# The end of a linear recurrence: a third panel over the finished channels, weights split into freed rooms, and the first evictions of the next stage

## The chip, the core and the metric

The kernel runs on one core of a Trainium2 chip. The metric is the device time of one execution in microseconds (us). A core has a matrix engine (TensorE, PE in the profile; PEld are its weight loads), a vector engine (VectorE, DVE), an activation engine (ScalarE, ACT), a general engine (GpSimd, POOL) and an engine that here only issues DMAs (SyncE, SP). They run side by side and wait for each other by semaphores; each takes its own instructions in order.

## What is computed

One layer of a streaming encoder, for a prompt of 1024 rows and a sample of 64 rows, which the kernel handles together as T = 1088 columns of transposed activations. Cut to what matters here:

```
z = rms_norm(x) @ w_in                      # xa, ga, q, k, v, gb, fl, ma, mb
ua = causal_conv(xa)                        # branch A, 1024 channels
r, i = sigmoid(blockdiag(ua) ...)
a = exp(-8 * r * softplus(-a_param))
h[t] = a[t] * h[t-1] + sqrt(1 - a[t]**2) * (i * ua)[t]     # the recurrence
ya = h * silu(ga)
yb = attention(q, k, v, forget) * silu(gb)  # branch B
u  = [ya @ w_branch[0], yb @ w_branch[1]]
mix = (sigmoid(ma) * u[0] + sigmoid(mb) * u[1]) @ w_o      # then norms, residual, a second small mix
```

All products are made in three passes of matmuls: each float32 operand is split into a high half (rounded on ACT) and a low half (the rest), and hi*hi, lo*hi and hi*lo are added up in one accumulator. So a weight panel is used only after a split: one ACT instruction writes wh, one DVE instruction writes wl.

## The kernel before

Channels of branch A are handled in eight tiles of 128 (k = 0 to 7, KT = 8). Weights come in panels of 128 output channels over eight tiles of input channels; over the 1088 columns a panel is three chunks of 364, 364 and 360 columns (CH), so 3 x 8 x 3 = 72 matmuls, and a chunk is 24. Each chunk has one accumulator; from the recurrence on there are eight of them, one PSUM bank each, taken in turn (`mm`, tag "acc").

`panel()` (L292) hands out the next panel in a fixed list: it asks for weights to be loaded when there is room (`look_ahead`, L257), splits them (`split_next`, L279), and also splits the panel after that, ahead of time. Raw weights lie in `w_raw`: two panels of branch A or B come as a pair in one load of four DMAs on SP, and the next pair is asked for only when both panels of the last are split. Split panels lie in wh and wl of `wpool`, two rooms each, so a new split waits for the matmuls of the panel two before it.

Recurrence (L1549 to L1642): for each k, a projection panel x (input), a panel g (SiLU gate), two small block matrices (`gate`, six accumulators gacc), then on ACT exponentials, tanh and a square root (`decay`, `root`), on DVE products and a scan (`state_in`, `scan`), the product with the gate (`output`), and the split of the result into ya[k] (`split_y`: yah on ACT, yal on DVE). The order on ACT and DVE is that of the code here (`manual_schedule`); PE's order is that of the code throughout. On POOL and SP, and on ACT and DVE behind L1642, a scheduler orders by its own estimate.

At the recurrence's end (k = 6 and 7) the code goes: the gate matmuls of 6, g6, the last merge-gate panel f (L1612, `fill`, evicted by `spill`: ACT copies to `st`, then stores to d_mb), the gate matmuls of 7 between f's first and second chunk, then g7 (L1620 and L1632). Behind it stand two panels of branch A's output projection that are held open (`Held`, L1532): a0 is taken at L1626 and a1 at L1644, each with three accumulators; they run over channels 0 to 4, then over channel 5, 6 and 7 as these get done. Channels 5, 6 and 7 (below y5, y6, y7) are split into rooms of tiles that the recurrence has finished with.

Then stage A (L1677): for of = 0 to 7, panel a_of over all channels, evicted by `evac_a`: DVE multiplies by the merge gate sigmoid(ma), which `gate_in` loads and passes through ACT one panel ahead, and SP stores to d_mix. `branch_b(of)` beside it makes one tile of branch B's y: two loads on SP (yb_in and gb_in, 544 KB each), a sigmoid on ACT, a product on POOL, one on DVE, then a split on ACT and DVE. Then stage B takes panels b0 to b7 over those.

The pools p3 (recurrence) and xpool are closed at L1649, and p4 and ybpool (stage A) take their memory: a tile there waits for the last use of what it lies over.

Of the kernel before, what the change touches and what calls it, by code (L numbers as in the profile page):

```python
# [7 lines left out]
F32 = mybir.dt.float32  # L8
F32R = mybir.dt.float32r
# [56 lines left out]
def hybrid_step(tc, a, o):  # L66
# [137 lines left out]
    def chunk(steps):  # L204
        for _ in range(KT):
            next(steps)
# [69 lines left out]
            for tag, raw in zip(tags, raws_):  # L276
                ahead.append([tag if isinstance(tag, tuple) else ("r", tag), raw, None, False, len(tags)])

    def split_next(eng):  # L279
        if ahead and ahead[0][2] is None:  # L280
            raw = ahead[0][1]
            wh = wpool.tile([P, KT, P], F32R, name="wh")
            wl = wpool.tile([P, KT, P], F32R, name="wl")
            copy_act(wh[:, :, :], raw)
            if ahead[0][0][0] in "xgf":
                copy_act(wl[:, :, :], f(wh[:, :, :]), -1.0)
                pool.dma_start(wl[:, :, :], raw, accum_op=ALU.add)
            else:
                sub(eng, wl[:, :, :], raw, f(wh[:, :, :]))
            ahead[0][2:4] = (wh, wl), True  # L290

    def panel(eng=None):  # L292

        look_ahead()
        if not ahead:
            return None
        split_next(eng or dve)
        tag, _, w, *_ = ahead.popleft()
        look_ahead()
        split_next(eng or dve)  # L300
        look_ahead()
        return tag, w

    def spill(dst, t0, n, z, s=None):
        s = s or wpool.tile([P, GC], F32, name="st")
        copy_act(s[:, :n], z)
        act.dma_start(dst[:, t0:t0 + n], s[:, :n])
# [1224 lines left out]
    class Held:  # L1532


        def __init__(self, want, xs):
            got, self.w = panel()
            assert got == want
            self.xs = xs
            self.accs = [mm.tile([P, 512], F32, name="held", tag="acc") for _ in CH]

        def part(self, ks, evac=None):
            for c, (t0, n) in enumerate(CH):
                for k in ks:
                    three(self.accs[c][:, :n], self.w[0][:, k, :], self.w[1][:, k, :],
                          self.xs[k][0][:, t0:t0 + n], self.xs[k][1][:, t0:t0 + n], k == 0, k == KT - 1)
                if evac:
                    evac(c, t0, n, self.accs[c][:, :n])
# [64 lines left out]
    tag, w = panel()  # L1612
    assert tag == ("f", KT - 1)
    fill = panel_steps(mm, *w, xs, lambda c, t0, n, z: spill(d_mb[KT - 1], t0, n, z))
    early_gate(k - 1)
    output(k - 1)
    chunk(fill)
    gate(k + 1)
    run(fill)
    ga = own_gate(k + 1)  # L1620
# [2 lines left out]
    decay(k + 1)  # L1623
    decay_a(k + 1)
    mix_u(k + 1)
    first = [Held(("a", 0), ya)]  # L1626
    root(k)
    root(k + 1)
    set_sigmoid()
    state(k)  # L1630
    output(k)
    run(ga)  # L1632
    state_in(k + 1)
    ya.append((shared('u', F32R, 'yah5'), shared('r', F32R, 'yal5')))
    split_y(5)
# [5 lines left out]
    split_y(7)  # L1641
    seq.__exit__(None, None, None)  # L1642
    first[0].part(range(5))
    first.append(Held(("a", 1), ya))  # L1644
    first[1].part(range(5))
    for i in (5, 6):
        for h in first:
            h.part([i])
    p3.close()  # L1649
    xpool.close()  # L1650

# [16 lines left out]
        sub(dve, l[:, :], t[:, :], f(h[:, :]))  # L1668

    def gate_in(pl, src):  # L1670
        g = pl.tile([P, T], F32, name="gate", tag="gate", bufs=2)
        sp.dma_start(g[:, :], src)
        act.activation(out=g[:, :], in_=g[:, :], func=AF.Sigmoid)
        return g

    g_next = gate_in(p4, d_ma[0])
    for of in range(KT):  # L1677
        g = g_next
        if of + 1 < KT:
            g_next = gate_in(p4, d_ma[of + 1])  # L1680

        def evac_a(c, t0, n, z):
            s = wpool.tile([P, GC], F32, name="st")
            dve.tensor_tensor(out=s[:, :n], in0=z, in1=g[:, t0:t0 + n], op=ALU.mult)
            sp.dma_start(d_mix[of][:, t0:t0 + n], s[:, :n])

        if of < 2:
            first[of].part([KT - 1], evac_a)
        else:
            tag, w = panel()  # L1690
            assert tag == ("a", of)
            run(panel_steps(mm, *w, ya, evac_a))
        branch_b(of)
        if of == 2:
            ft_p = mm.tile([P, 512], F32, name="ft_p", tag="acc")
            pe.transpose(ft_p[:64, :P], fin.rearrange("p s k -> p (s k)"), ident[:, :])
# [509 lines left out]
```

## Time and profile before

| | us |
|---|---|
| median of 3 runs (lowest, highest) | 1464.6 (1464.26, 1467.74) |
| the profiled execution | 1467.15 |
| its span | 1465.4 |
| mean granted TensorE clock over the span | 0.994 |

The profile is of one execution, so its times are compared with its own 1467.15 us. A row of a group of instructions gives the line in the code, the engine, the operation, written tile <- read tiles with shapes, the count, busy time and the mean of one; a row of the timeline begins with start and duration in us, and brackets at its end give how long the engine idled before it and what it waited for. Matmuls are pipelined: in an undisturbed stretch one of 364 columns is shown with 0.33 us and the next one starts 0.17 us later. The recurrence's end and the start of stage A lie between about 1010 and 1100 us of the span.

### The profile page before, as it was taken

The page shows a single profiled execution, that of the slowest core. Times are in us where ns is not written, and L with a number is a line of the kernel's source. Part 1 is how long each engine was busy: PE and PEld are TensorE (multiplying, and loading weights), DVE is VectorE, ACT ScalarE, POOL GpSimd, SP SyncE. Part 2 cuts the span into 40 slices and gives each one's busy share as a digit, 9 for nine tenths or more (in the row PEclk, how much of TensorE's full clock was granted, in tenths as well). Part 3 has the DMA queues.
Part 4 walks back from the last instruction along what each step waited for, and adds up shares of the span by engine and source line. Part 5 has one row for each costly group of instructions (what it writes and reads, how often), then busy time and mean ns, then how long its engine had stood idle before and what let it go on. Part 6 is the DMA issues. An engine that isn't in the chain of part 4 may idle for free.

```text
span 1465.4 us, 25652 instructions
## 1 busy us (share of the span) xinstructions
PE 1436.0 (98%) x9653; PEld 1394.7 (95%) x9653; DVE 893.7 (61%) x1631; ACT 717.1 (49%) x1353; POOL 299.1 (20%) x385
## 2 busy tenths in 40 slices
PE   8999999999999999999999999999999999999997
PEld 8999999999999999999899989999999999879997
DVE  5464866564325666666466555898755574778534
ACT  4423444442215566666456556777444232554633
POOL 0013324323123332333233210221023000000001
PEclk9999999999999999999999999999999999999999
DMA  8457456754276565646545344454278774224111
GB/s 285 143 119 109 130 163 189 181 178 127 78 210 157 120 148 139 141 112 139 118 129 128 61 108 70 86 101 84 99 235 273 257 218 152 100 86 171 43 43 44
DMA packets 149304, 200.64 MB, mean 137 GB/s; under 512 B 24212, under 2 KB 115836, under 8 KB 148156
## 3 DMA queue, kind: packets, MB, share of 16 engines
q1 hardware_dynamic: 129772, 167.06, 44.2%
q10 hardware_dynamic: 17680, 25.64, 5.1%
q0 software_dynamic: 1728, 6.29, 2.3%
q8 instruction: 76, 1.25, 0.4%
q14 instruction: 48, 0.39, 0.1%
HBM read 131.04 MB, written 65.80 MB: 134 GB/s over the span
## 4 chain that ended last, share of the span: by engine, by line
PE 84%; DVE 7%; ACT 4%; DMA 3%; issue 2%; SPq 0%; POOL 0%; ACTq 0%; DVEq 0%; POOLq 0%
PE quad L805 17%; PE acc L170 12%; PE acc L172 12%; PE acc L171 12%; PE q L1853 5%; PE tp L1147 4%; PE pv L1175 2%; PE s L1125 2%; PE s L1126 2%; PE pv L1177 2%; PE vacc L170 1%; PE vacc L171 1%; PE vacc L172 1%; PE vacc L471 1%; PE q L1978 1%
## 5 line engine op out<-in xcount | busy, mean ns | idle before, releaser
L170 PE MATMUL acc<-xh,wh 128*128 128x364 f32 (+1 forms) x768 | 253.2, 330 | 1.3 <-ACT st L82 1.2
L171 PE MATMUL acc<-xl,wh 128*128 128x364 f32 (+1 forms) x768 | 252.0, 328 | 0.0
L172 PE MATMUL acc<-xh,wl 128*128 128x364 f32 (+1 forms) x768 | 251.8, 328 | 0.0
L170 PEld LDWEIGHTS acc<-xh,wh 128*128 128x128 f32 x768 | 144.9, 189 | 2.6 <-ACT st L82 1.9
L171 PEld LDWEIGHTS acc<-xl,wh 128*128 128x128 f32 x768 | 144.7, 188 | 0.5
L172 PEld LDWEIGHTS acc<-xh,wl 128*128 128x128 f32 x768 | 144.5, 188 | 0.0
L1105 DVE CUSTOM_DVE_ANT_0 s<-s,mask 128x1024 f32<-128x1024 f32 (+7 forms) x128 | 95.5, 767 | 26.8 <-PE s L1126 26.7
L85 DVE TENSOR_TENSOR wl<-w_raw,wh 128x1024 fp32r<-128x1024 f32 (+1 forms) x54 | 62.6, 1160 | 67.3 <-ACT wh L82 66.3
L1110 POOL TENSOR_SCALAR pb<-pb,sm 128x896 f32<-128x896 f32 (+1 forms) x64 | 61.8, 966 | 196.2 <-DVE sm L1109 178.2
L82 ACT ACTIVATE wh<-w_raw 128x1024 fp32r<-128x1024 f32 (+1 forms) x66 | 64.3, 976 | 65.6 <-PE quad L805 27.3
L85 DVE TENSOR_TENSOR tl<-tp,th 128x512 fp32r<-128x512 f32 x96 | 65.7, 688 | 35.6 <-ACT th L82 35.6
L805 PE MATMUL quad<-xh,wh 128*128 128x272 f32 x384 | 80.7, 291 | 0.0
L805 PE MATMUL quad<-xl,wh 128*128 128x272 f32 x384 | 79.5, 288 | 0.0
L805 PE MATMUL quad<-xh,wl 128*128 128x272 f32 x384 | 79.4, 288 | 0.0
L82 ACT ACTIVATE th<-tp 128x512 fp32r<-128x512 f32 x96 | 56.9, 596 | 40.6 <-PE tp L1147 33.4
L1107 ACT ACTIVATE pb<-s,nm 128x896 f32<-128x896 f32 (+1 forms) x64 | 61.1, 954 | 30.0 <-DVE nm L1105 27.7
L1125 PE MATMUL s<-k,q 128*128 128x256 f32 (+1 forms) x192 | 67.1, 353 | 0.2 <-ACT pb L1107 0.2
L1147 PE MATMUL tp<-ident,pb 128*128 128x128 f32 x416 | 63.9, 274 | 1.2 <-DVE diag0l L85 0.7
L1126 PE MATMUL s<-k,q 68*128 68x256 f32 (+1 forms) x192 | 65.0, 350 | 0.0
L171 PE MATMUL acc<-ybl,wh 128*128 128x364 f32 (+1 forms) x192 | 62.9, 328 | 0.0
L172 PE MATMUL acc<-ybh,wl 128*128 128x364 f32 (+1 forms) x192 | 62.8, 327 | 0.0
L170 PE MATMUL acc<-ybh,wh 128*128 128x364 f32 (+1 forms) x192 | 62.7, 326 | 0.0
(705 smaller groups left out, 4151.8 us busy)
## 6 DMA issues: line engine op xcount, KB each, us to landing
w_raw<-in_w_in SPq DMA_DIRECT2D x56, 256.0 KB
q<-d_q SPq DMA_DIRECT2D x48, 256.0 KB
k<-d_k SPq DMA_DIRECT2D x48, 256.0 KB
w_raw<-in_w_in SPq DMA_DIRECT2D x64, 128.0 KB
w_raw<-in_w_branch SPq DMA_DIRECT2D x32, 256.0 KB
wl<-w_raw POOLq DMA_DIRECT2D x12, 512.0 KB, 4.6
wraw<-in_w_in SPq DMA_DIRECT2D x20, 256.0 KB
d_k<-oh ACTq DMA_DIRECT2D x16, 272.0 KB
```

The source lines that it names most:

```text
L82: return act.activation(out=out, in_=in_, func=AF.Copy, scale=scale)
L85: return eng.tensor_tensor(out=out, in0=in0, in1=in1, op=ALU.subtract)
L170: pe.matmul(out, ah, bh, start=start, stop=False)
L171: pe.matmul(out, ah, bl, start=False, stop=False)
L172: pe.matmul(out, al, bh, start=False, stop=stop)
L805: pe.matmul(acc[:, c, :CW], l[:, k, :], r[:, k, c * CW:(c + 1) * CW], start=(first and k == 0 and p == 0), stop=(k == 3 and p == 2), skip_ ...
L1105: at = book("D", now[0] + HOP_PE, per(D_MAX, n), lambda: dve.tensor_tensor_reduce(out=s[:, :n], in0=s[:, :n], in1=m, scale=-1.0, scalar=-N ...
L1110: return free, book("G", at, per(G_NORM, n), lambda: pool.tensor_scalar(out=pr[:, :n], in0=pr[:, :n], scalar1=sm, scalar2=1.0, op0=ALU.mul ...
L1125: pe.matmul(s[:, c0:c0 + w], t["q1"][:, q0:q0 + P], t["k1"][:, c0:c0 + w], start=True, stop=False)
L1126: pe.matmul(s[:, c0:c0 + w], t["q2"][:HD + 4, q0:q0 + P], t["k2"][:HD + 4, c0:c0 + w], start=False, stop=True)
L1147: pe.transpose(tp[:, o0 + i * P:o0 + (i + 1) * P], pr[par][:, kb * P:(kb + 1) * P], ident[:, :])
L1853: pe.matmul(acc, l[:, k, :], r[:, k, :], start=(first and k == 0 and i == 0), stop=(k == 3 and i == 2), skip_group_check=not first)
```

## The change

It has five parts.

1. f's first chunk (`chunk(fill)`) is written ahead of `early_gate` and `output` of channel 5, so that its eviction stands ahead of theirs on ACT and DVE.
2. `panel` may be given rooms for the panel that it splits ahead, and told not to split ahead. With a0, a1 is now split into the rooms uh and ul of p3 (inputs of the gate matmuls), no longer into wpool.
3. a1 and a2 are both taken inside the written order, behind g7 and ahead of `state_in(7)`; so a2 is split there too. a2 is held as well, with two accumulators, and its first two chunks run over channels 0 to 4, then 5, 6 and 7 with a0 and a1. `Held` takes an accumulator only when a chunk begins; a2's third chunk runs whole in stage A.
4. In stage A's first step, a3 is split and the pair a4 and a5 is asked for behind a0's last matmuls.
5. Evictions of stage A go to st_a of p4 with four rooms (before: st of wpool with two), and merge gates are loaded two panels ahead with three rooms (before: one ahead with two).

```diff
-    def split_next(eng):
+    def split_next(eng, rooms=None):
...
-            wh = wpool.tile([P, KT, P], F32R, name="wh")
-            wl = wpool.tile([P, KT, P], F32R, name="wl")
+            wh, wl = rooms or (wpool.tile([P, KT, P], F32R, name=n) for n in ("wh", "wl"))
...
-    def panel(eng=None):
+    def panel(eng=None, rooms=None, split=True):
...
-        split_next(eng or dve)
+        if split:
+            split_next(eng or dve, rooms)
...
-            self.accs = [mm.tile([P, 512], F32, name="held", tag="acc") for _ in CH]
-
-        def part(self, ks, evac=None):
-            for c, (t0, n) in enumerate(CH):
+            self.accs = {}
+
+        def part(self, ks, evac=None, cs=range(len(CH))):
+            for c in cs:
+                t0, n = CH[c]
+                if c not in self.accs:
+                    self.accs[c] = mm.tile([P, 512], F32, name="held", tag="acc")
...
+    chunk(fill)
     early_gate(k - 1)
     output(k - 1)
-    chunk(fill)
...
-    first = [Held(("a", 0), ya)]
+    rooms = [p3.tile([P, W_SC], F32R, name=n, tag=n)[:, :D].rearrange("p (k n) -> p k n", k=KT) for n in ("uh", "ul")]
+    first = [Held(("a", 0), ya, rooms=rooms)]
...
     run(ga)
+    first.append(Held(("a", 1), ya))
+    first.append(Held(("a", 2), ya, split=False))
     state_in(k + 1)
...
     first[0].part(range(5))
-    first.append(Held(("a", 1), ya))
     first[1].part(range(5))
+    first[2].part(range(5), cs=(0, 1))
     for i in (5, 6):
-        for h in first:
+        for h in first[:2]:
             h.part([i])
+        first[2].part([i], cs=(0, 1))
...
-        g = pl.tile([P, T], F32, name="gate", tag="gate", bufs=2)
+        g = pl.tile([P, T], F32, name="gate", tag="gate", bufs=3 if pl is p4 else 2)
...
-    g_next = gate_in(p4, d_ma[0])
+    g_ahead = deque(gate_in(p4, d_ma[i]) for i in range(2))
...
-            s = wpool.tile([P, GC], F32, name="st")
+            s = p4.tile([P, GC], F32, name="st_a", bufs=4)
...
         if of < 2:
             first[of].part([KT - 1], evac_a)
+            if of == 0:
+                split_next(dve)
+                look_ahead()
+        elif of == 2:
+            first[2].part([KT - 1], evac_a, (0, 1))
+            first[2].part(range(KT), evac_a, (2,))
```

How this moves instructions is seen in the built programs. First ACT, around the gate matmuls of channel 7; wh and wl are g7's weights, st is f's first chunk on its way out, q the sigmoid for channel 5's gate:

```order
 L82 ACTIVATE wh<-w_raw 128x1024
 L82 ACTIVATE wl<-wh 128x1024
+L82 ACTIVATE st<-acc 128x364
+L307 DMA d_mb<-st 128x364
 L1529 ACTIVATE q<-sg_e 128x1088
-L82 ACTIVATE st<-acc 128x364
-L307 DMA d_mb<-st 128x364
 L1444 ACTIVATE x_e<-gacc,vt 128x364 x3
```

The eviction and its store have moved ahead of the sigmoid. Next DVE, from channel 7's input product (x_e) to the last low half of y (the third yal is y7's). Before, where the first wl is a1's and the last a2's:

```order
L1450 TENSOR_TENSOR x_e<-x_e,u_e 128x1092
L85 TENSOR_TENSOR wl<-w_raw,wh 128x1024
L1478 SCALAR_TENSOR_TENSOR r<-e,r 128x1092
L1479 TENSOR_TENSOR x<-x,r 128x1092
L1480 COPY x<-vt 128x1
L1485 SCALAR_TENSOR_TENSOR e<-q,x 128x1092
L1503 TENSOR_TENSOR sg<-e,sg 128x1024
L1504 TENSOR_TENSOR sg<-e,sg 128x64
L1517 TENSOR_TENSOR sg_e<-acc,sg_e 128x364 x2
L1517 TENSOR_TENSOR sg_e<-acc,sg_e 128x360
L1478 SCALAR_TENSOR_TENSOR r_e<-e_e,r_e 128x1092
L1479 TENSOR_TENSOR x_e<-x_e,r_e 128x1092
```

And now, from the product with g7 on, where the first wl is a2's and the second a3's:

```order
L1517 TENSOR_TENSOR sg_e<-acc,sg_e 128x360
L85 TENSOR_TENSOR wl<-w_raw,wh 128x1024
L1478 SCALAR_TENSOR_TENSOR r_e<-e_e,r_e 128x1092
L1479 TENSOR_TENSOR x_e<-x_e,r_e 128x1092
L1480 COPY x_e<-vt 128x1
L85 TENSOR_TENSOR yal_12386<-xp,yah_12385 128x1088
L1485 SCALAR_TENSOR_TENSOR e_e<-q_e,x_e 128x1092
L1503 TENSOR_TENSOR r<-e_e,sg_e 128x1024
L1504 TENSOR_TENSOR r<-e_e,sg_e 128x64
L85 TENSOR_TENSOR yal_12396<-sg,yah_12395 128x1088
L85 TENSOR_TENSOR yal_12400<-r,yah_12399 128x1088
L85 TENSOR_TENSOR wl<-w_raw,wh 128x1024
```

a2's low half has come in ahead of channel 7's state; in a1's place, behind the first x_e, stands the same instruction with ul and uh for wl and wh. On ACT the high halves stand likewise: uh directly behind the tanh of channel 7, a2's wh ahead of y5's high half, and a3's behind y7's. Behind a3's low half DVE goes on with the first evictions into st_a. Third, SP at the start of stage A, with the semaphores that each request waits for. Before:

```order
L1672 DMA gate<-d_ma 128x1088 [waits DVE_49,PE_49,Pool_49]
L1672 DMA gate<-d_ma 128x1088
L1661 DMA yb_in<-d_y 128x1088 [waits DMAHW3_49]
L1662 DMA gb_in<-d_gb 128x1088 [waits DMAHW4_49,DVE_49]
L1685 DMA d_mix<-st 128x364 [waits DMAHW5_49,DVE_49]
```

And now:

```order
L1679 DMA gate<-d_ma 128x1088 [waits DVE_49,PE_49,Pool_49]
L1679 DMA gate<-d_ma 128x1088 [waits PE_49]
L1679 DMA gate<-d_ma 128x1088 [waits DMAHW3_49]
L1668 DMA yb_in<-d_y 128x1088 [waits DMAHW4_49,DVE_49,PE_49]
L1692 DMA d_mix<-st_a 128x364 [waits DMAHW5_49,DVE_49]
L1692 DMA d_mix<-st_a 128x364 [waits DMAHW6_49,DVE_49]
L1692 DMA d_mix<-st_a 128x360 [waits DMAHW7_49,DVE_49]
L254 DMA w_raw<-in_w_branch 128x2x256 [waits DMAHW0_49,Activation_49]
L254 DMA w_raw<-in_w_branch 128x2x256 [waits DMAHW1_49]
L254 DMA w_raw<-in_w_branch 128x2x256 [waits DMAHW2_49]
L254 DMA w_raw<-in_w_branch 128x2x256 [waits DMAHW3_49]
L1669 DMA gb_in<-d_gb 128x1088 [waits DMAHW4_49]
```

The second gate has gained a wait for PE: its room lies over uh, which a1's matmuls read to their end. Three gates now stand ahead of yb_in, and the first gb_in has moved behind a0's stores and the weights of a4 and a5. The DMAHW names stand for eight lanes that SP's requests take in turn; a request waits for the one eight before it. PE's order has the 30 matmuls of a2's first two chunks over channels 0 to 4 behind a1's, and 6 each for channels 5, 6 and 7; the rest of a2 follows behind a1's last matmuls.

More of the change, by code (lines that the diff above doesn't have):

```diff
@@ L1532, in hybrid_step, with __init__ @@
     class Held:
-        def __init__(self, want, xs):
-            got, self.w = panel()
+        def __init__(self, want, xs, **kw):
+            got, self.w = panel(**kw)
             assert got == want
             self.xs = xs
-            self.accs = [mm.tile([P, 512], F32, name="held", tag="acc") for _ in CH]
-        def part(self, ks, evac=None):
-            for c, (t0, n) in enumerate(CH):
+            self.accs = {}
[4 more added lines that the diff above has]
+                    self.accs[c] = mm.tile([P, 512], F32, name="held", tag="acc")
                 for k in ks:
@@ L1674, in gate_in @@
         return g
-    g_next = gate_in(p4, d_ma[0])
+    g_ahead = deque(gate_in(p4, d_ma[i]) for i in range(2))
     for of in range(KT):
-        g = g_next
-        if of + 1 < KT:
-            g_next = gate_in(p4, d_ma[of + 1])
+        g = g_ahead.popleft()
+        if of + 2 < KT:
+            g_ahead.append(gate_in(p4, d_ma[of + 2]))
         def evac_a(c, t0, n, z):
-            s = wpool.tile([P, GC], F32, name="st")
+            s = p4.tile([P, GC], F32, name="st_a", bufs=4)
             dve.tensor_tensor(out=s[:, :n], in0=z, in1=g[:, t0:t0 + n], op=ALU.mult)
```

## The prediction

> **What bounds the kernel now.** I read the page first, then the busy time by stage, then PE's own waits, then the rows around them. The page gives busy time and, in its chain, who ended last:
>
> ```profile
> PE 1436.0 (98%) x9653; PEld 1394.7 (95%) x9653; DVE 893.7 (61%) x1631; ACT 717.1 (49%) x1353; POOL 299.1 (20%) x385
> PE 84%; DVE 7%; ACT 4%; DMA 3%; issue 2%; SPq 0%; POOL 0%; ACTq 0%; DVEq 0%; POOLq 0%
> ```
>
> TensorE (PE) bounds the kernel nearly everywhere, so only PE's gaps can be won. By stage (us, then PE, PEld, DVE, ACT, POOL busy, clock, DMA share, GB/s), and PE's waits between 1000 and 1120 us:
>
> ```profile
> 1000.00:1050.00 50.00, 48.81 (x294) 48.51 (x293) 38.16 (x40) 32.89 (x47) 7.16 (x10) 1.00 0.33 83
> 1050.00:1100.00 50.00, 46.50 (x266) 45.30 (x265) 31.60 (x37) 18.60 (x18) 9.92 (x7) 0.97 0.65 216
> ```
>
> ```profile
> PE acc L172 <- DVE wl L85: 1.8, 1, 1.8
> PE held L171 <- DVE yal L85: 1.3, 2, 1.0
> PE acc L170 <- ACT st L82: 1.2, 1, 1.2
> PE held L170 <- ACT yah L82: 0.4, 1, 0.4
> ```
>
> The second stage's clock is 0.97: slices of 1 us show a half clock right after the last gap.
>
> ```profile
> 1069.00:1070.00 1.00, 1.00 (x6) 1.00 (x5) 1.00 (x2) 0.75 (x1) 0.00 (x0) 0.61 0.26 86
> 1071.00:1072.00 1.00, 1.00 (x5) 1.00 (x4) 0.16 (x1) 0.00 (x0) 0.00 (x0) 0.50 0.65 134
> 1072.00:1073.00 1.00, 1.00 (x5) 1.00 (x5) 1.00 (x2) 0.00 (x0) 0.00 (x0) 0.68 0.93 348
> ```
>
> What all this costs is counted between two matmuls, against the pace of an undisturbed stretch (start, duration; the last row is the stage after):
>
> ```profile
> 1018.21 0.33 PE L172 MATMUL gacc<-uh,g_l 128*128 128x364 f32 x1
> 1019.72 0.43 PE L170 MATMUL acc<-xh,wh 128*128 128x364 f32 x1 [1.19 <-ACT st L82]
> 1060.25 0.43 PE L171 MATMUL held<-yal,wh 128*128 128x364 f32 x1 [1.02 <-DVE yal L85]
> 1068.53 0.43 PE L172 MATMUL acc<-yah,wl 128*128 128x364 f32 x1 [1.85 <-DVE wl L85]
> 1081.82 0.27 PE L1696 MATMUL ft_p<-ident,fin 128*64 128x128 f32 x1
> 1082.00:1142.00 60.00, 60.00 (x362) 60.00 (x362) 33.23 (x36) 23.88 (x23) 16.67 (x6) 1.00 0.74 244
> ```
>
> Pace: 60.00 / 361 = 0.166 us. From 1019.72 to 1081.82 (62.1 us) lie 336 matmuls: two chunks of f (48), panel g7 (72), a0, a1 and a2 (72 each). They need 55.8 us; 6.3 are lost. Before them 1019.72 - 1018.21 - 0.17 = 1.3 are lost. **All that can be won here is 7.6 us**: idle 4.7 (the four waits), half clock 1.7 (0.39 + 0.50 + 0.50 + 0.32 of four slices, the second taken as the third), the rest five slow restarts.
>
> **The change part by part.** The times below are those of the profiled execution, whose 1467.15 us hold a span of 1465.4.
>
> *f's first chunk.* It ends early, but its eviction st stands behind the sigmoid q on ACT:
>
> ```profile
> 1018.21 1.09 ACT L1529 ACTIVATE q<-sg_e 128x1088 f32<-128x1088 f32 x1
> 1019.21 0.45 ACT L82 ACTIVATE st<-acc 128x364 f32<-128x364 f32 x1
> 1022.09 1.28 DVE L1530 TENSOR_TENSOR sg_e<-q,sg_e 128x1088 f32<-128x1088 f32 x1
> ```
>
> With q behind st, st runs 1018.21 to 1018.66 and PE resumes near 1018.72: 1.0 of the 1.3 goes, 0.35 stays. The sigmoid then ends near 1020.1; its reader on DVE, the third row, came at 1022.09 behind other work, which hides that. All PE work up to g7's end comes 1.0 earlier: wh in the next rows, which waited for that end, shows it at 1039.7; it becomes 1038.7.
>
> *a1 split into uh/ul.* Before, ACT waits for g7's matmuls to free a room, with the root of the last two channels queued behind:
>
> ```profile
> 1034.88 1.21 ACT L1458 ACTIVATE r_e<-r_e,sp 128x1092 f32<-128x1092 f32 x1
> 1039.74 1.06 ACT L82 ACTIVATE wh<-w_raw 128x1024 fp32r<-128x1024 f32 x1 [3.64 <-PE acc L171]
> 1038.23 1.29 DVE L1450 TENSOR_TENSOR x_e<-x_e,u_e 128x1092 f32<-128x1092 f32 x1
> 1043.26 1.30 DVE L1478 SCALAR_TENSOR_TENSOR r<-e,r 128x1092 f32<-128x1092 f32 x1 [1.20 <-ACT r L1474]
> ```
>
> The wait of 3.64 goes. DVE then binds: x_e ends at 1038.5 (all 1.0 earlier), a1's low half takes 1.2, so r starts near 1039.75 instead of 1043.26: 3.5 earlier.
>
> *a2 split before y5.* That adds one ACT and one DVE instruction ahead of the last channel's state; queued behind them are all of y5, y6 and y7. Its weights are asked for when a1's low half is done. Before, that was at 1042.05, and the transfer had ended by 1047.3:
>
> ```profile
> 1040.83 1.22 DVE L85 TENSOR_TENSOR wl<-w_raw,wh 128x1024 fp32r<-128x1024 f32 x1 [1.31 <-ACT wh L82]
> 1047.00:1048.00 1.00, 1.00 (x8) 1.00 (x7) 1.00 (x1) 0.82 (x1) 0.00 (x0) 1.00 0.31 107
> 1060.23 1.29 DVE L85 TENSOR_TENSOR yal<-r,yah 128x1088 fp32r<-128x1088 f32 x1
> ```
>
> So now asked at 1039.75, landed near 1045, split on ACT by 1046.1; DVE reaches it only near 1047.7, hence no wait. It costs 1.2 of the 3.5: y7 is whole near 1061.5 - 2.3 = 1059.2; y6, made just before it on DVE by the same operation, at 1057.9; y5 before both.
>
> *PE over finished channels.* From 1038.7: a0 and a1 with five channels 15.0 us, two chunks of a2 5.0 us, to 1058.7. Then y5 (24 matmuls, 4.0 us), y6 from 1062.7, y7 from 1066.7. All three are there 4.8 us or more ahead, so the waits on yah and yal (1.65) go. This cover is the 30 matmuls of a2; without it y6 and y7 would be late by about what they are now.
>
> *a3's split and a2's third chunk.* Before, a2's weights were split only when a0's were free:
>
> ```profile
> 1064.73 1.06 ACT L82 ACTIVATE wh<-w_raw 128x1024 fp32r<-128x1024 f32 x1 [4.54 <-PE held L171]
> 1064.87 2.52 POOL L1664 TENSOR_TENSOR yb_in<-yb_in,gb_in 128x1088 f32<-128x1088 f32 x1 [5.83 <-PE held L172]
> 1065.70 1.10 ACT L1673 ACTIVATE gate<-gate 128x1088 f32<-128x1088 f32 x1
> 1065.83 2.64 DVE L85 TENSOR_TENSOR wl<-w_raw,wh 128x1024 fp32r<-128x1024 f32 x1 [4.31 <-ACT wh L82]
> 1068.40 0.97 DVE L1684 TENSOR_TENSOR st<-held,gate 128x364 f32<-128x364 f32 x2
> 1069.29 1.21 DVE L85 TENSOR_TENSOR wl<-w_raw,wh 128x1024 fp32r<-128x1024 f32 x1
> ```
>
> Now that place is a3's, which PE needs 6 us later, so 1.85 and the half clock go. **A new wait takes its place**: all eight accumulators are held, and a2's third chunk needs a0's first eviction. That stands behind a3's low half on DVE. Call T the start of a0's last matmul (1068.05). ACT splits until T+1.3; gate 0 follows until T+2.3. DVE takes 1.2 (1069.29) to 2.6 (1065.83, with POOL multiplying beside it). Behind a3 POOL has nothing, since SP now asks for gb after the evictions; I take 1.2. The eviction ends at T+3.05; PE would go on at T+2.7. Loss 0.45, or 1.9 at the other end. With restarts, 1.0 of the 7.6 stays: **6.6 won so far**.
>
> *Transfers.* SP's second gate lies over uh now and waits for a1's last matmul, near 1069.7; all behind it on SP waits too. Before, this queue started at 1055.35:
>
> ```profile
> 1055.35 0.81 SPq L1672 DMA_DIRECT2D gate<-d_ma  x2
> gate<-d_ma SPq DMA_DIRECT2D x3, 544.0 KB
> 1075.00:1080.00 5.00, 5.00 (x32) 5.00 (x31) 3.11 (x4) 2.43 (x3) 2.74 (x1) 1.00 1.00 321
> 1080.00:1100.00 20.00, 20.00 (x123) 19.95 (x122) 10.02 (x14) 7.82 (x8) 3.23 (x2) 1.00 0.82 272
> ```
>
> Up to a6's weights SP issues some 22 transfers' worth of 544 KB (six gates, yb and gb of four panels, the stores of four panels, two pairs of weights of 1 MB each): 12.1 MB from 1070.9. At 272 / 0.82 = 332 GB/s they end at 1107.3; at 321 at 1108.6; at 272, with SP's waits, at 1115.4. a6 needs its halves at 1111.4, 2.5 after landing (ACT and DVE by the rows above): from 1.6 early to 6.5 late. With four rooms and gates two ahead SP waits less for evictions, so I take the nearer end, with 0.6 lost. a4's weights come in the first 3 MB: landed near 1081, needed at 1087.
>
> a5's and a7's halves come from the same two pairs, one panel of 12 us later. The request for a4 and a5 now goes out right behind a3's split, ahead of gb, which is what lets a4 keep its 6 us; the price is paid by yb and gb. These are needed last, at the start of branch B:
>
> ```profile
> 1139.76 1.29 DVE L85 TENSOR_TENSOR ybl<-yb_in,ybh 128x1088 fp32r<-128x1088 f32 x1 [0.73 <-ACT ybh L82]
> 1146.15 0.54 DVE L1787 TENSOR_TENSOR st<-acc,gate 128x364 f32<-128x364 f32 x1 [1.90 <-PE acc L172]
> ```
>
> Before, the last half of y in branch B was whole at 1141.05, and PE read it half a microsecond before its first chunk ended (1146.1): 4.5 to spare. Its request stands behind the stores of a6 as before, and PE's panels pace those; so it shifts with PE, and I count nothing. Without that slack each microsecond of lateness is one lost.
>
> **Sum: 7.6 - 1.0 - 0.6 = 6.0**, so 1467.15 becomes 1461.15. The runs shown have a median of 1464.6, 2.55 below the profiled execution; on that ground 1458.6, which I forecast.
>
> [...] The half clock above set in after gaps of 1.4 us (two together) and 1.85. [...]
>
> **The rivals.** (1) *The transfers pile up*: a6 waits 2 to 6.6 us. For it: share 1.00 and 0.82 in a stretch that was less crowded. Against it: SP's waits for evictions, which emptied the queue. It gives 1460 to 1464.6. (2) *Slower*: the same queue on a6, DMA below 275 GB/s through SP's waits; from a landing of 1115.5 on PE waits more than the change wins. At a wait of 10 us: 1468. (3) *Late eviction*: a3's low half at 2.6 and perhaps a half clock again: 1.4 to 3.1 more, 1460 to 1461.7. [...] (5) *It does not do what it says*: a2's weights come over 10 us after being asked, y5 to y7 slip behind them, and only the f term and a2's cover remain: 1462.
>
> **How the numbers follow.** Forecast (1457 to 1460) 0.50; (1) 0.20; (2) 0.07; (3) 0.10; (4) 0.08; (5) 0.05. The range takes in all 7.6 taken from the lowest run shown (1464.26), 1456.7, and (3), (4), (5) and most of (1), 1463.6. A measurement tells about 0.3%, 4.4 us, from no change: faster means below 1460.2. Faster: 0.50, half of (3) and (4) and a little of (1): 0.64. Slower beyond 1469 is part of (2): 0.05. Same: 0.31.
>
> **What would show it.** Right: the gap before f's second chunk near 0.3 us; a1's uh split directly behind r_e; no waits of held on yah or yal; clock 1.00 throughout 1060 to 1080; one short wait before a2's third chunk, on DVE. Wrong: PE waiting on wl or wh at a6, near 1111 us, with the DMA share near 1 ahead of it; a wl of 2.6 us before the first st_a; PE waiting on ybl at the start of branch B.

## The result, and the profile after

Over 14 runs each the median fell from 1467.45 us (1464.26 to 1468.82) to 1464.61 us (1462.39 to 1466.92): ratio 0.9981, 95% interval 0.9974 to 0.9989, a gain of 2.8 us (1.6 to 3.8) where 6.0 was forecast. The forecast's own base lay 2.85 us too low as well: by chance, two of the three runs shown are the two lowest of what became 14. So of the 6.0 us by which 1458.6 was missed, 2.85 are the base and 3.2 the gain.

First, where the prediction looked. These are PE's waits between 1000 and 1150 us in the profile after (total, times, longest), the busy time of the stages (as before: PE, PEld, DVE, ACT, POOL, clock, DMA share, GB/s), and the matmuls between which time is counted:

```profile
PE acc L171 <- DVE ybl L85: 0.9, 1, 0.9
PE acc L170 <- ACT st L82: 0.2, 1, 0.2
PE held L170 <- DVE st_a L1691: 0.2, 1, 0.2
PE acc L170 <- ACT ybh L82: 0.2, 1, 0.2
```

```profile
1050.00:1100.00 50.00, 49.80 (x300) 49.45 (x299) 26.96 (x35) 17.90 (x17) 8.74 (x6) 1.00 0.56 196
1100.00:1150.00 50.00, 48.92 (x292) 48.09 (x291) 27.72 (x34) 20.48 (x20) 17.31 (x6) 1.00 0.75 253
```

```profile
1020.61 0.33 PE L172 MATMUL gacc<-uh,g_l 128*128 128x364 f32 x1
1021.16 0.43 PE L170 MATMUL acc<-xh,wh 128*128 128x364 f32 x1 [0.23 <-ACT st L82]
1073.34 0.43 PE L170 MATMUL held<-yah,wh 128*128 128x360 f32 x1 [0.20 <-DVE st_a L1691]
1077.42 0.27 PE L1709 MATMUL ft_p<-ident,fin 128*64 128x128 f32 x1
1137.71 0.33 PE L170 MATMUL acc<-ybh,wh 128*128 128x364 f32 x1
1141.56 0.43 PE L170 MATMUL acc<-ybh,wh 128*128 128x364 f32 x1 [0.18 <-ACT ybh L82]
1142.88 0.44 PE L171 MATMUL acc<-ybl,wh 128*128 128x364 f32 x1 [0.90 <-DVE ybl L85]
```

The four old waits are gone and the clock is 1.00. From the last gacc to ft_p PE needs 56.81 us, against 1081.82 - 1018.21 = 63.61 before: 6.80 won, 6.6 forecast. Two things take it back in this pair of profiles.

The first is new: branch B's first chunk, 24 matmuls that took 4.00 us before, takes 5.62, since its last channel's halves are late. The chain of the page shows it too; before, no gb_in and no yb_in stood in that line:

```profile
PE quad L805 16%; PE acc L170 10%; PE acc L172 10%; PE acc L171 10%; PE tp L1147 4%; PE q L1866 4%; PE pv L1175 3%; PE s L1125 2%; PE pv L1177 2%; PE s L1126 2%; DMA gb_in<-d_gb 2%; PE vacc L170 1%; PE vacc L171 1%; PE vacc L172 1%; POOL yb_in L1671 1%
```

The second is not the change: the last gacc itself came at 1020.61 instead of 1018.21. The 2.4 us arose near 714 us, in code that both kernels share. The rows are PE's gap there, of before, of after and of a second profile of before, and then a slice of 2 us of before and of after:

```profile
713.48 0.38 PE L1175 MATMUL pv<-tl,vv 128*128 128x256 f32 x1 [3.32 <-DVE y L1186]
```

```profile
714.63 0.58 PE L1175 MATMUL pv<-tl,vv 128*128 128x256 f32 x1 [4.00 <-DVE y L1186]
```

```profile
713.29 0.58 PE L1175 MATMUL pv<-tl,vv 128*128 128x256 f32 x1 [3.87 <-DVE y L1186]
```

```profile
718.00:720.00 2.00, 2.00 (x14) 1.91 (x13) 0.76 (x2) 0.00 (x0) 0.80 (x1) 1.00 0.05 12
```

```profile
718.00:720.00 2.00, 2.00 (x8) 2.00 (x8) 1.29 (x2) 0.74 (x2) 0.54 (x1) 0.50 0.03 8
```

The second profile of before has the long gap too, and either kernel can have the shorter slow stretch or the longer one: matmuls of 364 columns start 0.30 us apart instead of 0.17, and the slow pace lasts from 714.9 to 718.4 in `c_after`, a later profile of the changed kernel, and from the gap's end at 716.6 to 721.5 in `e_f_only`, which is before with one edit. So this is chance between executions: a gap of 3.3 to 4.0 us, with a half clock of 3.4 us (before, from 714.2 us on) or of 6.8 (after, from 714.0 on). A difference of a few us between two single profiles therefore has to be read stage by stage.

### The profile page after: what moved, and what is told of

It is laid out like the page before. It is cut to its first block, busy times and chain, and to the rows that moved or that the text cites. A ratio compares the mean times of both kernels' runs of the same rounds, so it can differ in the third digit from the quotient of the medians.

```text
span 1463.1 us, 25647 instructions
## 1 busy us (share of the span) xinstructions
PE 1435.9 (98%) x9653; PEld 1394.3 (95%) x9653; DVE 890.9 (61%) x1631; ACT 717.6 (49%) x1353; POOL 301.8 (21%) x385
## 4 chain that ended last, share of the span: by engine, by line
PE 78%; DVE 7%; DMA 6%; ACT 4%; issue 2%; POOL 1%; SPq 1%; ACTq 0%; DVEq 0%; POOLq 0%
PE quad L805 16%; PE acc L170 10%; PE acc L172 10%; PE acc L171 10%; PE tp L1147 4%; PE q L1866 4%; PE pv L1175 3%; PE s L1125 2%; PE pv L1177 2%; PE s L1126 2%; DMA gb_in<-d_gb 2%; PE vacc L170 1%; PE vacc L171 1%; PE vacc L172 1%; POOL yb_in L1671 1%
```

## The experiments

The table gathers all runs; each number is a difference of two matmul starts in that kernel's profile. R: last gacc matmul to ft_p. A: ft_p to branch B's first matmul. B: branch B's first 24 matmuls. The ratio is to the kernel before beside it, with its 95% interval.

| run | R | A | B | sum | median us (runs) | ratio |
|---|---|---|---|---|---|---|
| before | 63.61 | 60.07 | 4.00 | 127.68 | 1467.45 (14) | |
| c_before | 61.21 | 60.23 | 4.00 | 125.44 | 1468.23 (12) | 1.0004 (0.9994-1.0014) |
| c_before_2 | 61.40 | 60.22 | 3.99 | 125.61 | 1464.85 (1) | |
| after | 56.81 | 60.29 | 5.62 | 122.72 | 1464.61 (14) | 0.9981 (0.9974-0.9989) |
| c_after | 56.79 | 61.82 | 5.39 | 124.00 | 1466.03 (12) | 0.9991 (0.9982-1.0000) |
| c_after_2 | 56.81 | 63.87 | 4.00 | 124.68 | 1466.32 (1) | |
| c_after_3 | 56.74 | 61.27 | 5.05 | 123.06 | 1464.92 (10) | 0.9983 (0.9972-0.9993) |
| e_f_only | 60.45 | 60.08 | 3.99 | 124.52 | 1465.90 (11) | 0.9986 (0.9977-0.9995) |
| e_before_yb_dve | 60.57 | 60.09 | 3.99 | 124.65 | 1466.00 (10) | 0.9985 (0.9973-0.9997) |
| e_no_third | 58.92 | 62.20 | 3.99 | 125.11 | 1464.97 (10) | 0.9987 (0.9978-0.9997) |
| e_no_gates | 56.74 | 62.92 | 7.20 | 126.86 | 1468.44 (10) | 1.0013 (1.0001-1.0025) |
| e_w_first | 56.82 | 60.07 | 9.87 | 126.76 | 1467.98 (10) | 1.0010 (1.0000-1.0019) |
| e_w_first, second profile | 56.89 | 60.07 | 9.06 | 126.02 | 1470.37 (1) | |
| e_yb7_dve | 56.72 | 60.29 | 4.73 | 121.74 | 1462.28 (5) | 0.9966 (0.9954-0.9978) |
| e_yb_dve | 56.79 | 60.07 | 4.00 | 120.86 | 1462.90 (5) | 0.9965 (0.9951-0.9979) |
| e_yb_dve_2 | 56.73 | 60.08 | 4.37 | 121.18 | 1461.61 (4) | 0.9957 (0.9941-0.9973) |
| e_yb_early | 56.78 | 60.08 | 3.99 | 120.85 | 1462.49 (12) | 0.9964 (0.9952-0.9976) |
| e_early_dve | 56.89 | 60.08 | 4.00 | 120.97 | 1461.74 (5) | 0.9960 (0.9945-0.9975) |

### Both kernels again

> The kernel before, once more, for a second profile and the granted clock of every run. Theory A (the change wins its 6.8 us between f's first chunk and branch A; the forecast's base was wrong, since two of the three runs shown were low ones): median 1467.0 to 1467.8, and a profile with the same four waits near 1019, 1060 and 1068 us. Rival B (the first profile was an unlucky execution and the four waits, or the half clock behind them, are smaller in most): a half clock near 1070 us is missing here, and the loss from the last gacc matmul near 1018 us to the matmul ft_p is under 6 us instead of 7.6.

> The kernel before, a third profile. Theory A: POOL's product meets a2's low half by another length again, the wait before a2 lies between 0.5 and 1.9 us, and the stage from the last gacc matmul to ft_p takes 61.0 to 61.9 us without a half clock there or 62.7 to 63.7 with one. Rival B (one of the two profiles was an exception): it equals one of the two to 0.1 us.

> The changed kernel, once more. Theory A: median 1464.2 to 1465.0; from the last gacc matmul to ft_p 56.8 us as in the first profile (63.6 in the one of before), and again a wait of 1 to 1.6 us on y's last channel in branch B near 1142 us; the gap near 712 us, in code the change does not touch, varies from run to run like that of the kernel before. Rival C (the change itself lengthens something outside its stage): the gap near 712 us is again 4.0 us with two slow stretches behind it, against 3.3 and one in the kernel before.

> The changed kernel, a third profile. Theory A: the stage from the last gacc matmul to ft_p takes 56.7 to 56.9 us again, whatever the rest does; a wait on ybl at branch B's start of 0.7 to 1.3 us; at a6 a wait of 0 or up to 1.5 us.

> The changed kernel beside these three: median 1464.3 to 1466, a wait on ybl of 0.7 to 1.3 at branch B's start, a6 waiting 0 to 1.8 us.

The first two medians missed what was expected: 1468.23 us for before (1467.0 to 1467.8) and 1466.03 for the changed kernel (1464.2 to 1465.0). The changed kernel's R is 56.7 to 56.8 every time. That of before is not fixed: 63.61, then 61.21 and 61.40, without a half clock. In those two the stage held 5.2 and 5.4 us to win (56.0 are needed), not 7.6: rival B was right on the size, and the third profile, with a wait of 1.2, is as theory A had it. The gap near 714 us was 3.9 us in each of these, of either kernel, with one slow stretch behind it in `c_after`, so rival C falls. What differs is the wait before a2. Here a2's low half on DVE, POOL's product beside it and the waiting matmul, in the second profile of before:

```profile
1065.35 1.89 DVE L85 TENSOR_TENSOR wl<-w_raw,wh 128x1024 fp32r<-128x1024 f32 x1 [4.31 <-ACT wh L82]
1063.61 2.54 POOL L1664 TENSOR_TENSOR yb_in<-yb_in,gb_in 128x1088 f32<-128x1088 f32 x1 [5.07 <-DMA gb_in<-d_gb]
1067.29 0.44 PE L172 MATMUL acc<-yah,wl 128*128 128x364 f32 x1 [1.09 <-DVE wl L85]
```

The same instruction took 2.64 in the first profile, where the two met for 1.56 us (from 1065.83 to 1067.39), and 1.89 here, where they met for 0.80. In both profiles this instruction, of 1.22 us elsewhere, is longer by nearly the time that the two run together: by 1.42 and by 0.67.

In A, the changed kernel loses another time in each profile: 0.2, 1.7, 3.8 and 1.2 us over the 60.08 of an undisturbed one, more than was expected of it; but for the 0.2, the loss is at a6. In c_after_2 the wait expected on ybl did not come: B is 4.00 there. In c_after_2 (SP's request of branch B's fourth channel, the DVE instruction that frees its room, POOL beside it, a6's weights asked for and split, and PE):

```profile
1101.89 0.32 SPq L1668 DMA_DIRECT2D yb_in<-d_y  x1
1098.45 3.41 DVE L85 TENSOR_TENSOR ybl<-yb_in,ybh 128x1088 fp32r<-128x1088 f32 x1
1098.17 2.54 POOL L1671 TENSOR_TENSOR yb_in<-yb_in,gb_in 128x1088 f32<-128x1088 f32 x1 [2.99 <-DVE wl L85]
1103.21 2.01 SPq L254 DMA_DIRECT2D w_raw<-in_w_branch  x4
1113.11 2.01 ACT L82 ACTIVATE wh<-w_raw 128x1024 fp32r<-128x1024 f32 x2 [0.97 <-DMA w_raw<-in_w_branch]
1114.22 0.44 PE L170 MATMUL acc<-yah,wh 128*128 128x364 f32 x1 [0.60 <-ACT wh L82]
1116.00 0.49 PE L172 MATMUL acc<-yah,wl 128*128 128x364 f32 x1 [1.18 <-DVE wl L85]
```

SP's request goes out at 1101.89, the moment after ybl ends (1101.86), which POOL stretched from 1.29 to 3.41; the weights stand behind it in SP's order. While the request waits, the DMA engines run half empty (share 0.47, the last number but one, in the first row below). Over the four profiles of the changed kernel, the first request for a6's weights goes out 23.9, 24.5, 25.5 and 25.8 us behind ft_p (after, c_after_3, c_after, c_after_2), and A loses 0.2, 1.2, 1.7 and 3.8. Of the 3.8, 1.7 are a half clock (0.38 + 0.50 + 0.50 + 0.32 of the four slices of 1 us from 1116 on, of which two are below):

```profile
1099.00:1103.00 4.00, 4.00 (x26) 4.00 (x26) 4.00 (x3) 0.25 (x1) 1.72 (x1) 1.00 0.47 160
1116.00:1117.00 1.00, 1.00 (x4) 1.00 (x5) 1.00 (x2) 0.00 (x0) 0.00 (x0) 0.62 1.01 401
1117.00:1118.00 1.00, 1.00 (x5) 1.00 (x4) 0.52 (x1) 0.07 (x1) 0.00 (x0) 0.50 1.06 388
```

### The first edit alone, and the product of before

```diff
+    chunk(fill)
     early_gate(k - 1)
     output(k - 1)
-    chunk(fill)
```

> The kernel before with the first edit alone: f's first chunk is issued ahead of the gate and the output of the channel before. Theory A: PE's gap there goes from 1.3 to 0.35 us, and the time falls by 1.0, to about 1466.4. Rival (what comes earlier waits at the next stage): the gap goes, but the waits on yal and wl near 1060 and 1068 us grow by as much, since y5 to y7 hang on DVE and not on PE, and the time stays.

R is 60.45, 0.85 below the two of before without a half clock; the waits behind it stay within what the profiles of before have (1.3 on yal, as there; 1.4 on wl, there 1.1 to 1.85). The f term stands; its median fits, with an interval that holds anything from 0.7 to 3.4 us.

```diff
-        pool.tensor_tensor(out=t[:, :], in0=t[:, :], in1=z[:, :], op=ALU.mult)
+        dve.tensor_tensor(out=t[:, :], in0=t[:, :], in1=z[:, :], op=ALU.mult)
```

> The kernel before, with the first product of branch B's y on DVE instead of POOL. Theory A (the 1.85 us before a2 in the first profile were the low half of a2's weights stretched from 1.22 to 2.64 us by POOL's product beside it, and how long they meet changes with the landing of gb): wl takes 1.2 us, PE's wait before a2 is 0.4 to 0.9 us, no half clock follows there, and the stage from the last gacc matmul to ft_p takes 60.5 to 61.2 us instead of 63.6 and 61.2; median 1466.0 to 1467.2. Rival E (the length of wl is the transfers' doing, not POOL's): wl still takes 1.9 to 2.6 us beside landing data, and the wait stays at 1.1 to 1.9.

```profile
1067.83 1.23 DVE L85 TENSOR_TENSOR wl<-w_raw,wh 128x1024 fp32r<-128x1024 f32 x1 [4.31 <-ACT wh L82]
1069.11 0.44 PE L172 MATMUL acc<-yah,wl 128*128 128x364 f32 x1 [0.42 <-DVE wl L85]
```

With POOL out of the way wl takes 1.23 and PE waits 0.42, at the low end of theory A; rival E falls. Three quarters of the 1.85 us in the first profile were POOL's doing.

### Parts of the change undone

`e_no_third` leaves out a2 as a held panel, and with it part 4 of the change (four places):

```diff
-    first.append(Held(("a", 2), ya, split=False))
...
-    first[2].part(range(5), cs=(0, 1))
...
-        first[2].part([i], cs=(0, 1))
...
-            if of == 0:
-                split_next(dve)
-                look_ahead()
-        elif of == 2:
-            first[2].part([KT - 1], evac_a, (0, 1))
-            first[2].part(range(KT), evac_a, (2,))
```

> The changed kernel without the third panel: a2 is not begun over finished channels and runs as a panel of its own, as before; the early split of a1 and the rooms stay. Theory A (the 30 matmuls of a2 are the cover of y6 and y7): PE waits on the halves of y6 and y7 again, 1.0 to 2.5 us in all near 1056 to 1063 us, the stage from the last gacc matmul to ft_p takes 58 to 60 us instead of 56.8; median 1 to 3 us above the changed kernel. Rival F (the early split of a1 alone brings y6 and y7 forward enough): the stage stays within 0.5 us of 56.8.

The waits on y6 and y7 are back (1.3 on yal and 0.4 on yah), R is 58.92: the cover of a2 is worth 2.1 us there, as theory A said. But theory A also had the median 1 to 3 us above that of the changed kernel, and it is not: B is 3.99 again. What the cover wins is lost behind it. A is 62.20, with a wait on a4's halves instead of a6's: without part 4 their weights are asked for 0.5 us behind ft_p, in the changed kernel 2.3 us ahead of it.

`e_no_gates` undoes part 5 of the change, which its expectation calls the third edit:

```diff
-        g = pl.tile([P, T], F32, name="gate", tag="gate", bufs=3 if pl is p4 else 2)
+        g = pl.tile([P, T], F32, name="gate", tag="gate", bufs=2)
...
-    g_ahead = deque(gate_in(p4, d_ma[i]) for i in range(2))
+    g_ahead = deque(gate_in(p4, d_ma[i]) for i in range(1))
...
-            s = p4.tile([P, GC], F32, name="st_a", bufs=4)
+            s = wpool.tile([P, GC], F32, name="st")
```

> The changed kernel with its third edit undone: one gate ahead in two rooms, evictions of branch A in the rooms that they shared with others. Theory A (this edit is not what sets the chain of branch B's y; it spares short waits of the evictions at most): the stage from the last gacc matmul to ft_p takes 56.8 to 57.6 us, the waits at a6 and at branch B's start stay (0 to 2, 0.5 to 1.5), median within 1.5 us of the changed kernel. Rival G (the gates asked for two ahead are what crowds out gb and the weights): the waits at a6 and on ybl go, and it is 1.5 to 3 us faster than the changed kernel.

Both were wrong: it is 1.7 us slower than before, by an interval that just excludes no change. R stays, but A and B take 2.6 and 1.6 us more than in the first profile of the changed kernel. Its waits between 1070 and 1150 us:

```profile
PE acc L170 <- ACT ybh L82: 1.4, 1, 1.4
PE acc L170 <- DVE st L1691: 1.3, 1, 1.3
PE acc L172 <- DVE wl L85: 1.0, 1, 1.0
PE acc L171 <- DVE ybl L85: 0.9, 1, 0.9
```

So part 5 keeps branch B's y from being later still; whether its rooms or its early gates do that is not told apart. The first product of branch B's y stands 0.4 us behind ft_p here, 8 us earlier than in the changed kernel, and the last channel is later all the same: an early start alone does not set the end.

### Which chain binds

```diff
             tag, w = panel()
             assert tag == ("a", of)
+            if of == 4:
+                branch_b(3)
             run(panel_steps(mm, *w, ya, evac_a))
-        branch_b(of)
+        if of != 3:
+            branch_b(of)
```

> The changed kernel, with the weights of a6 and a7 asked for ahead of the fourth channel of branch B's y on SP; POOL keeps its product. Theory A (SP's request for that channel waits for a room of yb_in, and the weights stand behind it): the weights are asked for by 24 us after ft_p in every profile, a6 does not wait; the wait on ybl at branch B's start stays at 0.5 to 1.3; median 1.0 to 2.0 us below the changed kernel. Rival D (bandwidth): the weights land no earlier, a6 waits in some profiles still, or branch B's start loses what a6 gains, and the time stays.

A second profile was taken of the same kernel:

> The kernel of the run before once more, for a second profile: no wait at a6 in this one either by theory A; up to 3.6 us there by the rival.

A is 60.07 in both, no wait at a6: the weights do stand behind that channel. But B takes 9.87 and 9.06, with a half clock of 6.8 us that sets in at 1142.7 us (in the second profile, the first matmul at that pace, of 0.67 us, starts at 1145.20), and the median is 1.2 us above that of before, at the edge of the noise. Theory A had the wait on ybl unchanged, and that is where it failed: what the weights gain, branch B's last two channels lose. Rival D had named that sign too, so this run does not separate the two. Waits from 1070 to 1150 us:

```profile
PE acc L171 <- DVE ybl L85: 2.5, 2, 1.7
PE acc L170 <- ACT ybh L82: 2.2, 1, 2.2
PE held L170 <- DVE st_a L1691: 0.2, 1, 0.2
```

This suggests that all eight channels of branch B's y form one chain, with two rooms, and that it binds; the next runs test it. In the changed kernel, SP's first requests, POOL's first and last product, and what SP's list of waits has for the second gate (total, times, longest):

```profile
1056.52 16.30 SPq L1679 DMA_DIRECT2D gate<-d_ma  x3
1072.93 0.36 SPq L1668 DMA_DIRECT2D yb_in<-d_y  x1
1079.84 0.34 SPq L1669 DMA_DIRECT2D gb_in<-d_gb  x1
1085.95 3.20 POOL L1671 TENSOR_TENSOR yb_in<-yb_in,gb_in 128x1088 f32<-128x1088 f32 x1 [25.73 <-DMA gb_in<-d_gb]
1135.34 3.69 POOL L1671 TENSOR_TENSOR yb_in<-yb_in,gb_in 128x1088 f32<-128x1088 f32 x1 [2.50 <-DMA gb_in<-d_gb]
```

```profile
SPq L1679 <- PE held L172: 15.3, 1, 15.3
```

Before, the first product stood at 1064.87, 17 us ahead of ft_p; now it stands at 1085.95, 8.5 us behind it. Seven periods then take 49.4 us, 7.1 each, and B loses 1.6. `e_yb_early` tests that start: channel 0 is asked for ahead of the second gate. For this, gb_s and a room of st_a are laid out first, so that the new requests lie off uh and ul. `load_b` is the first half of `branch_b`, its rooms and two loads; branch_b(0) and the first eviction then use b_first and st_first.

```diff
-    g_ahead = deque(gate_in(p4, d_ma[i]) for i in range(2))
+    g_ahead = deque([gate_in(p4, d_ma[0])])
+    st_first = p4.tile([P, GC], F32, name="st_a", bufs=4)
+    b_first = load_b(0)
+    g_ahead.append(gate_in(p4, d_ma[1]))
```

> The changed kernel, with the first channel of branch B's y and its gate asked for ahead of the second gate of branch A, in rooms that do not lie over those of a1's halves; POOL keeps the product. Theory A (the chain that makes the eight channels of branch B's y starts 20 us later than before, because its first request stands behind the second gate, which waits for a1's last matmul; what follows at a6 and at branch B's start is that lateness): POOL's first product starts before 1076 us instead of near 1086, the last one ends 2 us earlier or more against PE, the wait on ybl at branch B's start is under 0.4, a6 waits under 0.8 us, median 1.5 to 3 us below the changed kernel (1462 to 1463.5). Rival D (bandwidth and the two rooms of the chain set its end, wherever it starts): the last product ends where it did, the wait on ybl stays at 0.9, and the time stays.

```profile
1068.05 2.53 POOL L1675 TENSOR_TENSOR yb_in<-yb_in,gb_in 128x1088 f32<-128x1088 f32 x1 [8.60 <-DMA gb_in<-d_gb]
1133.61 2.95 POOL L1675 TENSOR_TENSOR yb_in<-yb_in,gb_in 128x1088 f32<-128x1088 f32 x1 [3.25 <-DMA gb_in<-d_gb]
1076.93 0.27 PE L1716 MATMUL ft_p<-ident,fin 128*64 128x128 f32 x1
```

Against ft_p the last product ends 2.0 us earlier (59.6 us behind it; 61.6 in the changed kernel). A is 60.08, B 3.99, and the median 2.4 us below that of the changed kernel beside it. Of the 17.4 us by which the chain starts earlier against ft_p, 2.0 reach its end, and they are enough. This run alone does not rule out bandwidth (rival D): the early request takes 1.1 MB out of a stretch in which the DMA engines are all but full (share 0.98 from 1080 to 1120 us in the changed kernel).

The other way is to shorten the chain itself, with the product on DVE: the edit above, for the last channel only (`e_yb7_dve`) or for all (`e_yb_dve`, twice).

> The changed kernel, with the first product of y's last channel in branch B on DVE instead of POOL (3.69 us there in the profile, about 1.3 on DVE). Theory A: that chain ends 1.5 to 2.5 us earlier, PE's waits at the start of branch B (0.18 and 0.90 us, with restarts 1.6) go or shrink below 0.3, and the median falls 1.2 to 1.6 below that of the changed kernel, to about 1463.2. Rival D (the channel is late because its data is late, not because of POOL): the wait stays above 0.8 us and the time stays.

> The changed kernel, with the first product of all eight channels of branch B's y on DVE instead of POOL. Theory A (after the change what binds from 1075 to 1143 us is the chain that makes branch B's y: SP's queue, gb's landing, the product, and DVE's instructions stretched from 1.22 to 2 or 3.5 us while POOL multiplies): no DVE instruction of that stage is over 1.4 us, no wait at a6, the wait at branch B's start goes or is under 0.5, median 1462.0 to 1463.5. Rival D (bandwidth binds: yb and gb land late because some 330 GB/s are all there is): the weights and gb land when they did, the wait on ybl stays at 0.9 and the time is that of the changed kernel.

> The changed kernel with the product on DVE, once more: theory A 1462 to 1463.5, no wait at a6; rival (the first five runs were lucky ones): within 1 us of the changed kernel beside it.

The last channel alone brings B to 4.73, a wait of 0.46 on ybl; that its profile has no wait at a6 can't be this edit's doing, which touches nothing ahead of it. Nor can all of its median, 3.7 us below that of the changed kernel beside it: B explains 0.3 to 0.9, and the rest is put down to chance (5 runs against 12). With all eight, no wl or ybl is over 1.4 us, a6 does not wait, and B is 4.00 and 4.37. In `e_yb_dve`, seven periods take 47.6 us instead of 49.4 and the last product 1.3 instead of 3.7, so it ends 57.7 us behind ft_p instead of 61.6. The median of `e_yb_dve_2` lies 3.3 us below the changed kernel beside it, so the first five runs were not just lucky. This kernel also answers rival D. Its transfers start as late as those of the changed kernel and keep the DMA engines as busy (share 0.98 and 0.99 in these 40 us of the two, whose ft_p lie 0.07 us apart), and in its profile nothing is lost:

```profile
1080.00:1120.00 40.00, 40.00 (x241) 39.72 (x240) 22.54 (x28) 19.51 (x18) 14.71 (x5) 1.00 0.98 349
1080.00:1120.00 40.00, 40.00 (x242) 40.00 (x241) 30.39 (x35) 20.30 (x19) 0.00 (x0) 1.00 0.99 353
```

So DMA engines that are full to 0.99 do not make A and B long by themselves here. How much of what the early request wins is the chain's start, and how much the emptier DMA engines, is not separated. Both remedies together:

> Both changes to that chain: the early request and the product on DVE. Theory A: no wait at a6 and none at branch B's start, stage from the last gacc matmul to ft_p 56.8 us; median 1461.5 to 1463, the best of the kernels tried. Rival H (DVE is then late for branch A's evictions, so PE waits for an accumulator): a wait on st_a of 0.5 us or more between 1070 and 1100 us, and no gain over the kernel with the product on DVE alone (1462.9).

They don't add up: either alone takes the lateness away, and the wait on st_a that rival H named is not there (0.2 us). At 1461.74 us it is 0.4% below the kernel before, not told apart from either remedy alone. The medians of `e_yb_early`, `e_early_dve` and `e_yb_dve_2` lie 2.4 to 3.3 us below the changed kernel beside them; all runs of the two with the product on DVE are below its lowest (1462.86), while those of `e_yb_early` reach into its range.

## Why the prediction was right or wrong

**f, a1, a2's cover: right.** The gap before f's second chunk is 0.23 us (0.35 forecast); the waits on yah and yal are gone, and leaving out a2's cover brings them back. One step on the way was off: the prediction had x_e come 1.0 us earlier with PE, but it starts 20.4 us behind the last gacc matmul, against 20.0 before. So r came 2.3 us earlier instead of 3.5, and y6 was there 3.6 us ahead of PE instead of 4.8; the margin hid it. **Third chunk: right**, 0.20 instead of 0.45. What stays of the loss in R is 0.8 us (1.0 forecast).

**"All that can be won here is 7.6 us": true of one execution only.** Against the other two profiles of before, the changed kernel wins 4.4 and 4.6, not 6.8. The rest was a half clock (1.7), and a longer meeting of wl with POOL's product (0.6 to 0.8). The prediction had a sign of it: it showed wl at 2.64 with POOL beside it and at 1.21 alone, and used that only for the range of the new wait, not for the one removed. This took 1.3 us from the gain: 5.3 in R on average, where 6.6 were forecast.

**Transfers, 0.6 lost at a6: mis-sized, and the reason was another.** Over four profiles A takes 61.81 us on average, against 60.17 before: 1.6 lost. Rival (1) came true in part, but not because 12 MB alone took too long: a request for yb waited for its room, with the weights behind it on SP.

**"It shifts with PE, and I count nothing": the step that failed.** The prediction said that SP's second gate would wait for a1's last matmul, that all behind it waits too, and that yb and gb pay. It then looked at the last channel only, and held that PE's panels pace its request. They don't. These are the changed kernel's last matmul of a6's third chunk, the ybl of the sixth channel, that chunk's eviction and store, and the last channel's request:

```profile
1125.56 0.32 PE L172 MATMUL acc<-yah,wl 128*128 128x360 f32 x1
1127.58 1.29 DVE L85 TENSOR_TENSOR ybl<-yb_in,ybh 128x1088 fp32r<-128x1088 f32 x1 [1.18 <-ACT ybh L82]
1128.78 0.53 DVE L1691 TENSOR_TENSOR st_a<-acc,gate 128x360 f32<-128x360 f32 x1
1129.34 0.32 SPq L1692 DMA_DIRECT2D d_mix<-st_a  x1
1129.75 0.44 SPq L1668 DMA_DIRECT2D yb_in<-d_y  x1
```

PE is done with the chunk near 1125.9, but its eviction stands on DVE behind that ybl, which waits for its own channel. In all four profiles the request goes out 0.88 us after the end of this ybl. In before it stood likewise 0.9 us behind the ybl of the seventh channel; there the chain had started early enough for this to cost nothing. So the channels ahead pace the last one, through two rooms and through DVE's order; started 25 us later against PE, the chain had no slack left. B takes 5.02 us on average instead of 4.00. The sign named for it, PE waiting on ybl at branch B's start, is there in three of four profiles.

Together: R wins 62.07 - 56.79 = 5.3, A loses 1.6, B 1.0; 2.6 us are left. Of the 3.4 us missing from 6.0, 1.3 are R, which had less to win in two of the three profiles of before; the other 2.0, 1.0 more at a6 than was counted and 1.0 at branch B, have that one late chain behind them. The three comparisons of medians gave 2.8, 1.3 and 2.9.

**The other rivals.** (2), slower, did not come, but e_w_first and e_no_gates show that the same chain can do it. (3), (5) and (4), by which the slow stretch would stay, did not come; that stretch left its old place (clock 1.00 from 1050 to 1150 us in the changed kernel's first profile), and in the changed kernel came back once, at a6. The 1.7 us of (4) are the half clock measured before; that something other than PE's gaps made it, no run shows. **The base**, 1464.6, was a median of three runs; later sets of 14 to 29 had 1466.8 to 1467.9.

## What to carry to other kernels

Price a step that goes earlier by what its memory was lent from: here two rooms taken for weights held back one gate, the gate held back SP's queue, and a chain of eight channels behind it lost a head start that no one had counted as slack. Where a chain with few rooms feeds a later stage, compare its start and its period with the date of its last link, not the last link's request alone. And before pricing a wait from one profile, ask whether what makes it long (an engine beside it, a clock stretch) is there in each execution.

## What the hardware showed

**DVE and POOL.** The product of 1088 columns takes POOL 2.5 us alone, and up to 3.7 beside DVE; DVE's subtraction, which reads two tiles, takes 1.2 to 1.3 alone, and 1.9 (c_before), 2.6 (before) and 3.4 (c_after_2) beside POOL. In these three the addition was 0.7 us at 0.80 us of overlap, 1.4 at 1.56, and 2.1 at 2.26 (1098.45 to 1100.71), while POOL, which had begun first, kept its 2.5. Where DVE's subtraction had begun first (after, at 1085.52 and 1098.67), it kept its 1.23 and 1.28, and POOL took 3.20 and 3.63, which is 0.7 and 1.1 more at overlaps of 0.80 and 1.23. With the product on DVE the addition is gone: 1.23 in e_before_yb_dve, at most 1.29 in e_yb_dve. So in each of these five the one that started second was longer, by nearly the overlap, and the first kept its time; what in the two engines makes it so, no run shows.

**The clock.** Between 60 and 1450 us, the profiles of before and after have three half clocks: near 714 us in both, with gaps of 3.32 and 4.00 us, and from 1069.2 in before, behind the gap of 1.85; their other gaps there, up to 1.19 us, had none. At a6 in c_after_2 a half clock followed gaps of 0.60 and 1.18 us within 2.4 us; in c_before and c_before_2 gaps of 1.09 and 1.2 brought none, nor did 1.43 in c_after or the first gap, of 1.65, in e_w_first. So the length of a single gap does not tell which brings one; what sets the limit, no run here tells.
